# Solving the triangular systems of two DeltaNet heads together, with the keys' norms taken ahead

## The chip, the cores and the metric

The kernel runs on one core of a Trainium2 chip. The metric is the device time of one execution in microseconds (us). Each core has TensorE (PE, matrix products into PSUM), VectorE (DVE), ScalarE (ACT), GpSimd (POOL) and SyncE (SP, which issues the DMAs). Each engine works through its own instructions in the order in which they are written, and engines wait for each other by semaphores.

## The reference, cut to what matters

One layer of a diffusion backbone on 512 latent and 256 context tokens of width 1024. One projection feeds two mixers, a gated DeltaNet of 8 heads and an mLSTM of 4 heads, both run forward and backward in time; they are gated, projected, merged and normalised. The change touches the DeltaNet. Per head, chunk and direction it needs the inverse of a unit lower triangular matrix:

```python
kb = kc * bc[..., None]
a = jnp.where(strict, jnp.einsum('nbhid,nbhjd->nbhij', kb, kc) * dmask, 0.0)
eye = jnp.eye(CHUNK, dtype=a.dtype)
tinv = lax.linalg.triangular_solve(a + eye, jnp.broadcast_to(eye, a.shape),
                                   left_side=True, lower=True)
u = jnp.einsum('nbhij,nbhjd->nbhid', tinv, vc * bc[..., None])
w = jnp.einsum('nbhij,nbhjd->nbhid', tinv, kb * jnp.exp(gcum)[..., None])
```

The keys k are divided by their norm before this (`l2norm`).

## The kernel before

The kernel takes chunks of 128 tokens: 6 of them, 2 of context and 4 latent (NCH = 6). The projections are dense products of 128x128 weights with 512 or 256 tokens, three fp32r products each (weights and activations are split into a high and a low part: `whs`/`wls`, `hh`/`hl`). ScalarE makes `whs` and VectorE `wls` for each block of weights. They fill TensorE most of the time, and the DeltaNet's steps are set between them.

The steps of one DeltaNet head are generators. `dn_kv` transposes the keys and values and makes the squared norms `ssk`, and from them C1 (the factor beta over the squared norm), C1E and nk. `dn_scores` makes the decay mask Dm (ScalarE's exponential of a TensorE product) and multiplies it with the products q k and k k; the latter, GD, overwrites Dm. Dm has two buffers; that of head h is free after the last product with GD in `dn_prepb(h)`. `dn_prepa2` inverts the diagonal blocks: each 128x128 matrix has 4 diagonal blocks of 32x32, so that a head has 6 x 4 = 24 blocks in each of 2 directions. VectorE multiplies the blocks of GD with C1 into `TC2` (8 products), two 32x32 stream transposes lay them out in `TL` with one block on each partition, and 30 substitution steps follow, each a product into `tmp` and a subtraction. Here 64 partitions hold the blocks (32 for each direction), and the other 64 hold the same blocks for the odd columns: `Z` has the even columns on partitions 0 to 63 and the odd on 64 to 127. ScalarE copies to this layout and back, GpSimd clears the upper part and sets the diagonal, and two more transposes leave the inverses in `TL`.

`dn_prepb` places the inverted blocks from TL into A1, B1 and XF (ScalarE and GpSimd) and puts together the inverse of the 128x128 matrix by products on TensorE: first A1 with GD, then W with B1, then the same with A2 and B2. `dn_scan` runs 6 steps over the chunks in both directions; `dn_norm` and `dn_out` end the head.

The loop over the heads puts a stage together: `dn_prepb(h)` beside `dn_kv(h + 1)`, then the scan of h beside `dn_prepa2(h + 1)` and `dn_scores(h + 2)`, and beside all of it dense work (`z_dense`, `ml_dense`, `ml_gate`, `qkv(h + 3)`) and at odd heads `ml_mix`, the mLSTM.

What is recorded in this way is not yet the program. A `Recorder` takes each instruction with its reads and writes, and `_arrange` sets the order on each engine: a list scheduling over a table of costs in ns (`_cost`), by how urgent an instruction is for TensorE (`_needs`), in 8 rounds of which it keeps the one that its costs like best. So a change in one step can move instructions of every engine. All instructions that were recorded have line 460 in the profile; tiles tell them apart.

Of the kernel before, what the change touches and what calls it, by code (L numbers as in the profile page):

```python
# [21 lines left out]
NCH = TT // P  # L22
# [466 lines left out]
def conv_col(ch):  # L489
    return ch * P if ch < NCC else SEG + (ch - NCC) * P  # L490


def hybrid(tc, x, c, ctx_in, c_ctx, ada_w, ada_b, norm_g, w_in, conv_w, a_log, dt_bias,
           norm_a_g, i_bias, f_bias, norm_b_g, w_pa, w_pb, w_out, final_g, out):
    nc = tc.nc
# [9 lines left out]
    hs = ExitStack()  # L505
# [51 lines left out]
    cpow = const.tile([P, 16], F32, name="cpow")[:, 0:2]  # L557
# [46 lines left out]
    nc = rec  # L604
# [8 lines left out]
    gch, gcl, bcol, NEGC, EKD, EGL, KW, BB, EM, SCL = [rec.wrap(t) for t in gcols]  # L613
# [13 lines left out]
    pt = psm()  # L627
# [18 lines left out]
    junk = sp.tile([P, D], F32, name="junk")  # L646
# [57 lines left out]
    for half in range(2):  # L704
# [288 lines left out]
    def zeroed(name, shape):  # L993
        t = mx.tile(shape, F32, name=name)
        nc.gpsimd.memset(t, 0.0)
        return t

    TL = zeroed("TL", [P, 32, 32])
    TC2 = zeroed("TC2", [64, 32, 32])
    A1 = zeroed("A1", [P, NCH, P])  # L1000
    B1 = zeroed("B1", [P, NCH, P])
    A2, B2 = A1, B1
# [27 lines left out]
    heads = {}  # L1030
# [33 lines left out]
    def transposes(src, cols, pt=None):  # L1064
        pt = pt or psm()
        for i, cl in enumerate(cols):
            nc.tensor.transpose(pt[:, P * i:P * i + P], src[:, cl:cl + P], ident)
        return pt

    BATCH = ((0, 3), (3, 6))  # L1070

    def dn_kv(h):

        r = heads[h]
        k, v = r["k"], r["v"]
        KTm = mx.tile([P, NCH, P], F32, tag="KT", name="KTm", bufs=2)
        Vt = mx.tile([P, NCH, P], F32, tag="Vt", name="Vt", bufs=2)
        ssk = mx.tile([P, NCH], F32, tag="ssk", name="ssk", bufs=2)
        for b0, b1 in BATCH:
            pt = transposes(k, [conv_col(ch) for ch in range(b0, b1)], psl())  # L1080
            n = b1 - b0
            nc.scalar.copy(KTm[:, b0:b1, :], pt[:, 0:n * P].rearrange("p (c i) -> p c i", i=P))
            for ch in range(b0, b1):
                nc.scalar.activation(Vt[:, ch, :], KTm[:, ch, :], AF.Square, accum_out=ssk[:, ch:ch + 1])
            yield Y_T
        rk2 = mx.tile([P, NCH], F32, tag="rk2", name="rk2", bufs=2)
        nk = mx.tile([P, NCH], F32, tag="nk", name="nk", bufs=2)
        nc.vector.tensor_scalar(ssk, ssk, EPS, None, op0=ALU.add)
        nc.vector.reciprocal(rk2, ssk)
        nc.gpsimd.tensor_tensor(nk, ssk, cpow[:, 1:2].broadcast_to([P, NCH]), op=ALU.pow)  # L1090
        C1 = mx.tile([P, 2, NCH], F32, tag="C1", name="C1", bufs=2)
        C1E = mx.tile([P, 2, NCH], F32, tag="C1E", name="C1E", bufs=2)
        for d in range(2):
            nc.vector.tensor_tensor(C1[:, d, :], bcol[:, :, 8 * d + h], rk2, op=ALU.mult)
            nc.vector.tensor_tensor(C1E[:, d, :], C1[:, d, :], EKD[:, :, 8 * d + h], op=ALU.mult)
        yield Y_T
        for b0, b1 in BATCH:
            pt = transposes(v, [conv_col(ch) for ch in range(b0, b1)], psl())
            for ch in range(b0, b1):
                nc.scalar.activation(Vt[:, ch, :], pt[:, P * (ch - b0):P * (ch - b0) + P], AF.Copy, scale=nk[:, ch:ch + 1])  # L1100
            yield Y_T
        r.update(KT=KTm, Vt=Vt, C1=C1, C1E=C1E)

    def dn_scores(h):

# [39 lines left out]
            yield Y_T  # L1145
        r.update(GD=GD, PD=PD)

    def dn_prepa2(h):
        r = heads[h]
        C1, GD = r["C1"], r["GD"]  # L1150

        for b in range(4):
            sl = slice(32 * b, 32 * b + 32)
            for d in range(2):
                nc.vector.tensor_tensor(TC2[32 * d:32 * d + 32, 6 * b:6 * b + 6, :], GD[sl, :, sl],
                                        C1[sl, d, :].unsqueeze(2).broadcast_to([32, NCH, 32]), op=ALU.mult)
        nc.vector.transpose(TL[0:32], TC2[0:32].rearrange("p l i -> p i l"))
        nc.vector.transpose(TL[32:64].rearrange("p r c -> p c r"), TC2[32:64].rearrange("p l i -> p i l"))

        nc.scalar.copy(TL[64:128], TL[0:64])  # L1160
        Z = mx.tile([P, 32, 16], F32, tag="Z", name="Z")
        nc.scalar.copy(Z[0:64], TL[0:64, :, 0:32:2])
        nc.scalar.copy(Z[64:128], TL[0:64, :, 1:32:2])
        nc.vector.memset(Z[64:128].rearrange("p a b -> p (a b)")[:, 16:512:33], 0.0)
        tmp = mx.tile([P, 128], F32, tag="tmp", name="tmp")
        for s in range(1, 31):
            m, w = 31 - s, (s + 1) // 2
            tv = tmp[:, 0:m * w].rearrange("p (r c) -> p r c", c=w)
            nc.vector.tensor_tensor(tv, TL[:, s + 1:32, s:s + 1].broadcast_to([P, m, w]),
                                    Z[:, s:s + 1, 0:w].broadcast_to([P, m, w]), op=ALU.mult)  # L1170
            nc.vector.tensor_tensor(Z[:, s + 1:32, 0:w], Z[:, s + 1:32, 0:w], tv, op=ALU.subtract)
            if s % 5 == 0:
                yield Y_I
        nc.scalar.copy(TC2[:, :, 0:32:2], Z[0:64])
        nc.scalar.copy(TC2[:, :, 1:32:2], Z[64:128])
        nc.gpsimd.affine_select(out=TC2, in_=TC2, pattern=[[1, 32], [-1, 32]], compare_op=ALU.is_gt,
                                fill=0.0, base=0, channel_multiplier=0)
        nc.gpsimd.memset(TC2.rearrange("p a b -> p (a b)")[:, 0:1024:33], -1.0)
        nc.vector.transpose(TL[0:64].rearrange("p l s -> p s l"), TC2)
        nc.vector.transpose(TL[64:128].rearrange("p l s -> p s l"), TC2.rearrange("p r c -> p c r"))  # L1180
        yield Y_I

    def dn_prepb(h):
        r = heads[h]
        k, q, C1, GD, PD = r["k"], r["q"], r["C1"], r["GD"], r["PD"]
        Xf, Xb, XfT, XbT = TL[0:32], TL[96:128], TL[64:96], TL[32:64]

        def placep(dst, src, b, b0=0, b1=NCH):
            sl = slice(32 * b, 32 * b + 32)
# [7 lines left out]
        for b in range(4):  # L1197
            sl = slice(32 * b, 32 * b + 32)
# [11 lines left out]
        for b in (1, 2):  # L1210
            sl = slice(32 * b, 32 * b + 32)
# [53 lines left out]
        pt = psm()  # L1265
# [264 lines left out]
    for h in range(HA):  # L1530
        j = h // 2
        last = h + 1 == HA
        p1, p2 = [(W_B, dn_prepb(h))], [(W_S + W_N, seq(dn_scan(h), dn_norm(h), dn_out(h)))]
        if h + 1 < HA:
            p1.append((W_KV, dn_kv(h + 1)))
            p2.append((W_A2, dn_prepa2(h + 1)))
        if h + 2 < HA:
            p2.append((W_E, dn_scores(h + 2)))
        dn, wd = [par(*p1), par(*p2)], sum(w for w, _ in p1 + p2)
        de, cost = [], 0.0  # L1540
        if h + 1 < HA:
# [26 lines left out]
    nc, ps_d, ps_l, ps_s, ps_o, wpool, cvp, hh, hl, whs, wls, ya_d, yb_d, sg_d, gate_d, cpow = plain  # L1568
# [35 lines left out]
    for n in range(KT):  # L1604
        terms = []
        for i, ((ph, pl), wsrc) in enumerate(((parts[1], w_pa[0]), (parts[0], w_pb[0]))):
# [4 lines left out]
            w = load_w(wsrc, P * n)  # L1611
# [34 lines left out]
    n = [0] * NLC  # L1646
    for i, c0, c1 in pieces:
        wh, wl = wo[c0 // HD]
        cs, w0, w = slice(c0, c1), c0 % HD, c1 - c0
        ps = psd()[:, 0:w]  # L1650
        m = 0
# [12 lines left out]
        r = rf[:, i:i + 1]  # L1664
# [34 lines left out]
```

## Time and profile before

| | |
|---|---|
| median of 3 runs | 1000.65 us (1000.18 to 1001.67) |
| profiled execution | 1000.94 us, its span 999.2 us |
| TensorE busy | 956.1 us (96%) |
| VectorE busy | 741.1 us (74%) |
| ScalarE busy | 537.9 us (54%) |
| GpSimd busy | 214.5 us (21%) |
| mean granted TensorE clock | 0.989 of 2.4 GHz |

Times in the rows are us unless marked ns. A tile's buffer numbers are left out, so TC is TC2, A is A1, and so on. An fp32 product of TensorE stands as two records, an fp32r product or a transpose as one. The granted clock is 1.00 at 2.4 GHz and 0.5 at 1.2 GHz; a share between them is a mean over a stretch.

### The profile page before, as it was taken

The page shows a single profiled execution, that of the slowest core. Times are in us where ns is not written, and L with a number is a line of the kernel's source. Part 1 is how long each engine was busy: PE and PEld are TensorE (multiplying, and loading weights), DVE is VectorE, ACT ScalarE, POOL GpSimd, SP SyncE. Part 2 cuts the span into 40 slices and gives each one's busy share as a digit, 9 for nine tenths or more (in the row PEclk, how much of TensorE's full clock was granted, in tenths as well). Part 3 has the DMA queues.
Part 4 walks back from the last instruction along what each step waited for, and adds up shares of the span by engine and source line. Part 5 has one row for each costly group of instructions (what it writes and reads, how often), then busy time and mean ns, then how long its engine had stood idle before and what let it go on. Part 6 is the DMA issues. An engine that isn't in the chain of part 4 may idle for free.

```text
span 999.2 us, 15245 instructions
## 1 busy us (share of the span) xinstructions
PE 956.1 (96%) x5504; PEld 816.6 (82%) x5504; DVE 741.1 (74%) x1694; ACT 537.9 (54%) x1181; POOL 214.5 (21%) x292
## 2 busy tenths in 40 slices
PE   4999999999999899999989999999999999999996
PEld 2288889778889689988878998887998888788875
DVE  5798877887868978887888787887878445543544
ACT  6467564864775475485456558536545434422322
POOL 2201130411430151142023124103014000011131
PEclk9999999999999899999998999999999999999999
DMA  9821321533411231332114024214245148654462
GB/s 274 265 64 43 88 65 43 148 106 85 117 44 43 74 84 43 86 95 65 43 32 127 22 64 118 62 32 112 80 91 115 46 109 251 182 148 135 141 175 84
DMA packets 133104, 99.93 MB, mean 100 GB/s; under 512 B 6488, under 2 KB 113155, under 8 KB 133029
## 3 DMA queue, kind: packets, MB, share of 16 engines
q1 hardware_dynamic: 133029, 98.96, 35.9%
q8 instruction: 43, 0.70, 0.3%
q14 instruction: 32, 0.26, 0.1%
HBM read 89.70 MB, written 9.24 MB: 99 GB/s over the span
## 4 chain that ended last, share of the span: by engine, by line
PE 81%; DVE 8%; DMA 5%; ACT 4%; issue 1%; POOL 1%; SPq 0%; POOLq 0%; DVEq 0%; ACTq 0%
PE psd L460 46%; PE psl L460 16%; PE pts L460 6%; PE psd L769 3%; PE psd L770 3%; PE psd L768 3%; PE ops L460 3%; PE psd L1654 2%; DMA raw<-in_w_out 1%; DVE TL L460 1%; DMA xt<-in_x 1%; DMA yld<-ya_d 1%; DMA yld<-yb_d 1%; DVE xn L460 1%; DVE wls L460 1%
## 5 line engine op out<-in xcount | busy, mean ns | idle before, releaser
L460 PE MATMUL psd<-hh,whs 128*128 128x512 f32 (+1 forms) x696 | 273.6, 393 | 4.9 <-ACT pad L460 1.9
L460 PE MATMUL psd<-hh,wls 128*128 128x512 f32 (+1 forms) x696 | 259.2, 373 | 1.5 <-DVE wls L460 1.5
L460 PE MATMUL psd<-hl,whs 128*128 128x512 f32 (+1 forms) x696 | 258.6, 372 | 0.0
L460 PEld LDWEIGHTS psd<-hh,whs 128*128 128x128 f32 x696 | 132.2, 190 | 23.0 <-ACT pad L460 2.4
L460 PEld LDWEIGHTS psd<-hh,wls 128*128 128x128 f32 x696 | 131.7, 189 | 23.3 <-DVE wls L460 2.4
L460 PEld LDWEIGHTS psd<-hl,whs 128*128 128x128 f32 x696 | 132.3, 190 | 17.6 <-issue 0.9
L460 DVE TENSOR_TENSOR wls<-raw,whs 128x1024 fp32r<-128x1024 f32 x83 | 106.5, 1285 | 13.1 <-ACT whs L460 12.5
L460 ACT CAST whs<-raw 128x1024 fp32r<-128x1024 f32 x83 | 86.6, 1049 | 29.6 <-PE psd L460 16.8
L460 DVE STREAM_TRANSPOSE TL<-TC 32x1024 f32<-32x1024 f32 (+1 forms) x32 | 67.1, 2098 | 0.7 <-POOL TC L460 0.2
L460 DVE TENSOR_TENSOR Z<-Z,tmp 128x30 f32<-128x30 f32 (+7 forms) x240 | 62.4, 260 | 5.8
L460 DVE TENSOR_TENSOR tmp<-TL,Z 128x30 f32<-128x30 f32 (+7 forms) x240 | 61.7, 257 | 5.4
L460 ACT ACTIVATE ud<-pts,C1E 128x128 f32<-128x128 f32 x80 | 27.9, 366 | 55.4 <-PE pts L460 55.1
L460 PE MATMUL psd<-whs,hh 128*128 128x256 f32 x192 | 56.3, 294 | 0.0
L460 PE MATMUL psd<-wls,hh 128*128 128x256 f32 x192 | 54.6, 284 | 0.0
L460 PE MATMUL psd<-whs,hl 128*128 128x256 f32 x192 | 54.4, 284 | 0.0
L460 POOL TENSOR_SCALAR_AFFINE_SELECT Mm<-gch 128x384 fp32r<-128x384 f32 x32 | 22.7, 709 | 145.3 <-PE psl L460 110.7
L460 ACT ACT_TABLE_LOAD x40 | 51.3, 1283 | 1.5 <-PEq L1687 0.8
L753 ACT CAST whs<-raw 128x1024 fp32r<-128x1024 f32 x21 | 22.1, 1052 | 48.1 <-PE psd L769 44.0
L1615 POOL TENSOR_TENSOR yt<-yt 128x512 f32<-128x512 f32 x8 | 14.7, 1831 | 106.5 <-DVE yt L1613 71.4
L754 DVE TENSOR_TENSOR wls<-raw,whs 128x1024 fp32r<-128x1024 f32 x21 | 27.9, 1328 | 12.7 <-ACT whs L753 11.4
L460 POOL TENSOR_SCALAR_AFFINE_SELECT P<-PD 128x512 f32<-128x512 f32 x8 | 6.6, 827 | 142.6 <-PE ops L460 137.5
L460 PEld LDWEIGHTS psd<-wls,hh 128*128 128x128 f32 x192 | 36.6, 191 | 0.1
(299 smaller groups left out, 2217.0 us busy)
## 6 DMA issues: line engine op xcount, KB each, us to landing
raw<-in_w_in SPq DMA_DIRECT2D x80, 512.0 KB, 3.9
ada_t<-in_ada_w SPq DMA_DIRECT2D x16, 512.0 KB, 9.5
raw<-in_ada_w SPq DMA_DIRECT2D x8, 512.0 KB, 3.7
Qd<-rows_d SPq DMA_DIRECT2D x16, 256.0 KB, 4.2
raw<-in_w_pa SPq DMA_DIRECT2D x8, 512.0 KB, 3.8
raw<-in_w_pb SPq DMA_DIRECT2D x8, 512.0 KB, 3.9
raw<-in_w_out SPq DMA_DIRECT2D x8, 512.0 KB, 8.9
sg_d<-sg SPq DMA_DIRECT2D x11, 256.0 KB, 3.2
```

The source lines that it names most:

```text
L460: getattr(getattr(self.nc, s.eng), s.name)(*a, **k)
L753: nc.scalar.copy(wh, raw)
L754: nc.vector.tensor_tensor(wl, raw, wh.bitcast(F32), op=ALU.subtract)
L768: nc.tensor.matmul(o, wh[:, kt, :], rh[:, kt, t0:t1], start=kt == 0, stop=False)
L769: nc.tensor.matmul(o, wh[:, kt, :], rl[:, kt, t0:t1], start=False, stop=False)
L770: nc.tensor.matmul(o, wl[:, kt, :], rh[:, kt, t0:t1], start=False, stop=kt == KT - 1)
L1615: nc.gpsimd.tensor_tensor(terms[0], terms[0], terms[1], op=ALU.add)
L1654: nc.tensor.matmul(ps, a[:, kt, P * i:P * i + P], b[:, kt, w0:w0 + w], start=m == 0, stop=m == KT * 3 - 1)
```

## The change

`dn_prepa2` takes one or two heads. Each head has 64 partitions of `TL` (32 for each direction) and keeps whole columns, so that Z, the split by column parity and ScalarE's copies are gone; the substitution runs in place in TL, with `tmp` up to 240 columns wide. The blocks are laid out through `TX`. The two transposes at the end move into `dn_prepb`, from TL into TX, so that TL keeps a second head's inverses until its own `dn_prepb`.

The heads go as 0 alone, then 1 and 2, 3 and 4, 5 and 6, and 7 alone. At even h the loop solves h+1 and h+2 after `dn_scores(h + 2)`; at odd h it solves nothing. Since C1 of head h+2 is now needed a stage earlier, `dn_norms(h + 2)` transposes its keys only for their norms; `dn_kv` transposes them again later for the scan, without the norms. C1 and C1E have three buffers instead of two.

```diff
+    def dn_norms(h):
+
+        ssk = mx.tile([P, NCH], F32, tag="ssk", name="ssk", bufs=2)
+        for b0, b1 in BATCH:
+            pt = transposes(heads[h]["k"], [conv_col(ch) for ch in range(b0, b1)], psl())
+            for ch in range(b0, b1):
+                junk = mx.tile([P, P], F32, tag="u", name="junk", bufs=2)
+                nc.scalar.activation(junk, pt[:, P * (ch - b0):P * (ch - b0) + P], AF.Square, accum_out=ssk[:, ch:ch + 1])
+            yield Y_T
+        dn_factors(h, ssk)
+        yield Y_T
...
-    def dn_prepa2(h):
...
-        nc.scalar.copy(TL[64:128], TL[0:64])
-        Z = mx.tile([P, 32, 16], F32, tag="Z", name="Z")
-        nc.scalar.copy(Z[0:64], TL[0:64, :, 0:32:2])
-        nc.scalar.copy(Z[64:128], TL[0:64, :, 1:32:2])
...
+    def dn_prepa2(*hs):
+
+
+        n = 64 * len(hs)
+        nc.gpsimd.memset(TX[0:n, 24:32, :], 0.0)
+        for e, h in enumerate(hs):
+            C1, GD = heads[h]["C1"], heads[h]["GD"]
+            heads[h]["inv"] = e
+            for b in range(4):
+                sl = slice(32 * b, 32 * b + 32)
+                for d in range(2):
+                    q = 64 * e + 32 * d
+                    nc.vector.tensor_tensor(TX[q:q + 32, 6 * b:6 * b + 6, :], GD[sl, :, sl],
+                                            C1[sl, d, :].unsqueeze(2).broadcast_to([32, NCH, 32]), op=ALU.mult)
+            q = 64 * e
+            nc.vector.transpose(TL[q:q + 32], TX[q:q + 32].rearrange("p l i -> p i l"))
+            nc.vector.transpose(TL[q + 32:q + 64].rearrange("p r c -> p c r"), TX[q + 32:q + 64].rearrange("p l i -> p i l"))
+        tmp = mx.tile([P, 240], F32, tag="tmp", name="tmp")
         for s in range(1, 31):
-            m, w = 31 - s, (s + 1) // 2
...
+            m = 31 - s
+            tv = tmp[0:n, 0:m * s].rearrange("p (r c) -> p r c", c=s)
+            nc.vector.tensor_tensor(tv, TL[0:n, s + 1:32, s:s + 1].broadcast_to([n, m, s]),
+                                    TL[0:n, s:s + 1, 0:s].broadcast_to([n, m, s]), op=ALU.mult)
+            nc.vector.tensor_tensor(TL[0:n, s + 1:32, 0:s], TL[0:n, s + 1:32, 0:s], tv, op=ALU.subtract)
...
     def dn_prepb(h):
...
-        Xf, Xb, XfT, XbT = TL[0:32], TL[96:128], TL[64:96], TL[32:64]
+        z = TL[64 * r["inv"]:64 * r["inv"] + 64]
+        nc.vector.transpose(TX[0:64].rearrange("p l s -> p s l"), z)
+        nc.vector.transpose(TX[64:128].rearrange("p l s -> p s l"), z.rearrange("p r c -> p c r"))
+        Xf, Xb, XfT, XbT = TX[0:32], TX[96:128], TX[64:96], TX[32:64]
...
-            p2.append((W_A2, dn_prepa2(h + 1)))
-        if h + 2 < HA:
-            p2.append((W_E, dn_scores(h + 2)))
+        if h + 2 < HA:
+            early = [dn_norms(h + 2), dn_scores(h + 2), dn_prepa2(h + 1, h + 2)] if h % 2 == 0 else [dn_scores(h + 2)]
+            p2.append((3 * Y_T + W_E + W_A2 if h % 2 == 0 else W_E, seq(*early)))
+        elif h + 1 < HA:
+            p2.append((W_A2, dn_prepa2(h + 1)))
```

How the scheduler's order moves is shown at two places. First VectorE ahead of the solve that `dn_prepb(3)` needs. Before, the block products of head 3 alone (TC) are made right after its factors C, and the scores of head 4 are not among the rows ahead:

```order
L460 TENSOR_TENSOR C_3713<-bcol,rk_3639 128x6
L460 TENSOR_TENSOR TC_617<-Dm,C_3713 32x192 x8
L460 SCALAR_TENSOR_TENSOR cvv<-pad_117,cwt,cvv 128x772
L460 STREAM_TRANSPOSE TL<-TC_617 32x1024
L460 SCALAR_TENSOR_TENSOR Sn<-Sn,EGL,pts 128x128 x2
L460 TENSOR_TENSOR wls<-raw,whs 128x1024
L460 SCALAR_TENSOR_TENSOR R<-pts,NEGC,Vt 128x128 x2
L460 STREAM_TRANSPOSE TL<-TC_617 32x32x32
```

Now the score products of head 4 (Dm from psl, which is GD) stand straight ahead of its block products (TX), and these ahead of the solve of heads 3 and 4:

```order
L460 TENSOR_TENSOR wls<-raw,whs 128x1024
L460 SCALAR_TENSOR_TENSOR Sn<-Sn,EGL,pts 128x128
L460 TENSOR_TENSOR Dm<-psl,Dm 128x384 x2
L460 TENSOR_TENSOR TX<-Dm,C_3720 32x192
L460 SCALAR_TENSOR_TENSOR R<-pts,NEGC,Vt 128x128 x2
L460 TENSOR_TENSOR TX<-Dm,C_3720 32x192 x7
L460 STREAM_TRANSPOSE TL<-TX 32x1024
L460 TENSOR_TENSOR wls<-raw,whs 128x1024
L460 STREAM_TRANSPOSE TL<-TX 32x32x32
L460 TENSOR_TENSOR kw<-psl,KW 128x384 x2
```

So the scores of the later head have moved in front of the earlier head's solve. The second place is TensorE at `dn_prepb(1)`. Before, transposes (mk, cvk), products of the mLSTM (mq) and dense products (psd) stand between the products with A and B:

```order
L460 MATMUL psd<-hh,wls 128x512
L460 MATMUL psl<-A_637,Dm 128x128 x3
L460 MATMUL psl<-ident,mk 128x128 x3
L460 MATMUL psl<-ident,cvk 128x128 x3
L460 MATMUL psl<-A_637,Dm 128x128 x3
L460 MATMUL psd<-hh,whs 128x512
L460 MATMUL psd<-hl,whs 128x512
L460 MATMUL psl<-B_642,W 128x128 x3
L460 MATMUL psl<-mq,mk 128x128 x4
L460 MATMUL psl<-B_642,W 128x128 x3
```

Now they follow the transposes of head 0's output (on), and one another, almost alone:

```order
L460 MATMUL psd<-hh,wls 128x512
L460 MATMUL psl<-ident,on 128x128 x4
L460 MATMUL psl<-A_639,Dm 128x128 x6
L460 MATMUL psl<-B_647,W 128x128 x6
L460 MATMUL psd<-hh,whs 128x512
L460 MATMUL psd<-hl,whs 128x512
L460 MATMUL psl<-A_639,Dm 128x128 x3
L460 MATMUL psl<-ident,cvv 128x128 x3
L460 MATMUL psl<-mV,kw 128x257
L460 MATMUL psl<-A_639,Dm 128x128 x3
```

The dense work that stood between them has moved to other places of the queue.

## Rows read from the trace of the kernel before

**Rows 1.** The page, busy time of each engine, its share of the span, instructions:
```profile
PE 956.1 (96%) x5504; PEld 816.6 (82%) x5504; DVE 741.1 (74%) x1694; ACT 537.9 (54%) x1181; POOL 214.5 (21%) x292
```
**Rows 2.** The page, the chain that ended last, shares of the span:
```profile
PE 81%; DVE 8%; DMA 5%; ACT 4%; issue 1%; POOL 1%; SPq 0%; POOLq 0%; DVEq 0%; ACTq 0%
```
**Rows 3.** Stretch of the scans: length, busy us of each engine, clock, DMA:
```profile
175.00:775.00 600.00, 582.41 (x3591) 513.79 (x3591) 499.08 (x1214) 360.27 (x885) 152.98 (x219) 0.99 0.30 79
```
**Rows 4.** Two stretches with a low clock (the third number from the end):
```profile
275.00:350.00 75.00, 68.88 (x389) 60.54 (x388) 61.20 (x176) 42.19 (x92) 14.51 (x22) 0.93 0.20 54
500.00:550.00 50.00, 44.25 (x256) 38.60 (x256) 43.78 (x91) 30.42 (x90) 15.13 (x24) 0.93 0.29 80
```
**Rows 5.** Waits of TensorE, 175 to 775 us: us, times, longest:
```profile
PE psl L460 <- DVE A L460: 5.6, 4, 2.7
PE psl L460 <- DVE Z L460: 3.1, 1, 3.1
```
**Rows 6.** VectorE, groups by shape: count, busy us, mean ns, idle before:
```profile
L460 DVE TENSOR_TENSOR wls<-raw,whs 128x1024 fp32r<-128x1024 f32 x83 | 106.5, 1285 | 13.1 <-ACT whs L460 12.5
L460 DVE STREAM_TRANSPOSE TL<-TC 32x1024 f32<-32x1024 f32 x16 | 33.8, 2115 | 0.3
L460 DVE SCALAR_TENSOR_TENSOR cvk<-pad,cwt,cvk 128x772 f32<-128x772 f32 x32 | 33.5, 1047 | 2.2 <-ACT cvk L460 1.9
L460 DVE STREAM_TRANSPOSE TL<-TC 64x1024 f32<-64x1024 f32 x16 | 33.3, 2082 | 0.4 <-POOL TC L460 0.2
L460 DVE SCALAR_TENSOR_TENSOR R<-pts,NEGC,Vt 128x128 f32<-128x128 f32 x80 | 25.1, 346 | 15.0 <-PE pts L460 14.4
L460 DVE TENSOR_TENSOR TC<-Dm,C 32x192 f32<-32x192 f32 x64 | 24.8, 387 | 1.1
L460 DVE TENSOR_SCALAR wts<-wts,BB 128x128 f32<-128x128 f32 x32 | 9.4, 347 | 0.1
L460 DVE TENSOR_TENSOR kw<-psl,KW 128x384 f32<-128x384 f32 x16 | 8.2, 548 | 1.0 <-PE psl L460 0.9
L460 DVE TENSOR_TENSOR tmp<-TL,Z 128x120 f32<-128x120 f32 x24 | 7.3, 304 | 0.5
L460 DVE TENSOR_TENSOR tmp<-TL,Z 128x30 f32<-128x30 f32 x16 | 3.5, 216 | 0.3
```
**Rows 7.** ScalarE, groups by shape, the copies around a solve:
```profile
L460 ACT COPY Z<-TL 64x512 f32<-64x512 f32 x16 | 10.5, 659 | 0.2
L460 ACT COPY TC<-Z 64x512 f32<-64x512 f32 x16 | 10.5, 655 | 13.8 <-DVE Z L460 13.6
L460 ACT COPY TL<-TL 64x1024 f32<-64x1024 f32 x8 | 8.4, 1046 | 10.5 <-DVE TL L460 10.5
```
**Rows 8.** GpSimd, groups by shape, the select after a solve:
```profile
L460 POOL TENSOR_SCALAR_AFFINE_SELECT TC<-TC 64x1024 f32<-64x1024 f32 x8 | 10.7, 1343 | 80.8 <-ACT TC L460 80.8
```
**Rows 9.** TensorE in order of time: start, length, records (an A product has two):
```profile
273.63 0.39 PE L460 MATMUL psd<-hh,whs 128*128 128x512 f32 x1
273.86 0.39 PE L460 MATMUL psd<-hl,whs 128*128 128x512 f32 x1
...
276.82 0.28 PE L460 MATMUL psd<-hh,wls 128*128 128x256 f32 x1
276.94 0.83 PE L460 MATMUL psl<-A,Dm 128*128 128x128 f32 x6
277.61 0.49 PE L460 MATMUL psl<-ident,cvv 128*128 128x128 f32 x3
```
**Rows 10.** VectorE in order of time, seven block products of head 7:
```profile
705.71 2.54 DVE L460 TENSOR_TENSOR TC<-Dm,C 32x192 f32<-32x192 f32 x7
```
**Rows 11.** TensorE in order of time, first A and last B products of head 2:
```profile
356.88 0.83 PE L460 MATMUL psl<-A,Dm 128*128 128x128 f32 x6
...
368.45 0.92 PE L460 MATMUL psl<-B,W 128*128 128x128 f32 x6
```

More of the change, by code (lines that the diff above doesn't have):

```diff
@@ L998, in hybrid @@
     TL = zeroed("TL", [P, 32, 32])
-    TC2 = zeroed("TC2", [64, 32, 32])
+    TX = zeroed("TX", [P, 32, 32])
     A1 = zeroed("A1", [P, NCH, P])
@@ L1070, in hybrid, with dn_factors @@
     BATCH = ((0, 3), (3, 6))
+    def dn_factors(h, ssk):
+        rk2 = mx.tile([P, NCH], F32, tag="rk2", name="rk2", bufs=2)
+        nk = mx.tile([P, NCH], F32, tag="nk", name="nk", bufs=2)
+        nc.vector.tensor_scalar(ssk, ssk, EPS, None, op0=ALU.add)
+        nc.vector.reciprocal(rk2, ssk)
+        nc.gpsimd.tensor_tensor(nk, ssk, cpow[:, 1:2].broadcast_to([P, NCH]), op=ALU.pow)
+        C1 = mx.tile([P, 2, NCH], F32, tag="C1", name="C1", bufs=3)
+        C1E = mx.tile([P, 2, NCH], F32, tag="C1E", name="C1E", bufs=3)
+        for d in range(2):
+            nc.vector.tensor_tensor(C1[:, d, :], bcol[:, :, 8 * d + h], rk2, op=ALU.mult)
+            nc.vector.tensor_tensor(C1E[:, d, :], C1[:, d, :], EKD[:, :, 8 * d + h], op=ALU.mult)
+        heads[h].update(C1=C1, C1E=C1E, nk=nk)
+    def dn_norms(h):
[8 more added lines that the diff above has]
+        yield Y_T
     def dn_kv(h):
@@ L1077, in dn_kv @@
         Vt = mx.tile([P, NCH, P], F32, tag="Vt", name="Vt", bufs=2)
-        ssk = mx.tile([P, NCH], F32, tag="ssk", name="ssk", bufs=2)
+        if "C1" not in r:
+            ssk = mx.tile([P, NCH], F32, tag="ssk", name="ssk", bufs=2)
         for b0, b1 in BATCH:
@@ L1082, in dn_kv @@
             nc.scalar.copy(KTm[:, b0:b1, :], pt[:, 0:n * P].rearrange("p (c i) -> p c i", i=P))
-            for ch in range(b0, b1):
-                nc.scalar.activation(Vt[:, ch, :], KTm[:, ch, :], AF.Square, accum_out=ssk[:, ch:ch + 1])
+            if "C1" not in r:
+                for ch in range(b0, b1):
+                    nc.scalar.activation(Vt[:, ch, :], KTm[:, ch, :], AF.Square, accum_out=ssk[:, ch:ch + 1])
             yield Y_T
[L1086 to L1095, printed above, removed]
+        if "C1" not in r:
+            dn_factors(h, ssk)
+        nk = r["nk"]
         yield Y_T
@@ L1101, in dn_kv @@
             yield Y_T
-        r.update(KT=KTm, Vt=Vt, C1=C1, C1E=C1E)
+        r.update(KT=KTm, Vt=Vt)
     def dn_scores(h):
@@ L1146, in dn_scores @@
         r.update(GD=GD, PD=PD)
-    def dn_prepa2(h):
[L1149 to L1158, printed above, removed]
-        nc.scalar.copy(TL[64:128], TL[0:64])
-        Z = mx.tile([P, 32, 16], F32, tag="Z", name="Z")
-        nc.scalar.copy(Z[0:64], TL[0:64, :, 0:32:2])
-        nc.scalar.copy(Z[64:128], TL[0:64, :, 1:32:2])
-        nc.vector.memset(Z[64:128].rearrange("p a b -> p (a b)")[:, 16:512:33], 0.0)
-        tmp = mx.tile([P, 128], F32, tag="tmp", name="tmp")
-        for s in range(1, 31):
-            m, w = 31 - s, (s + 1) // 2
[L1168 to L1171, printed above, removed]
@@ new lines, in dn_prepa2 @@
+    def dn_prepa2(*hs):
[6 more added lines that the diff above has]
+                sl = slice(32 * b, 32 * b + 32)
+                for d in range(2):
+                    q = 64 * e + 32 * d
[5 more added lines that the diff above has]
+        tmp = mx.tile([P, 240], F32, tag="tmp", name="tmp")
+        for s in range(1, 31):
+            m = 31 - s
[3 more added lines that the diff above has]
+            nc.vector.tensor_tensor(TL[0:n, s + 1:32, 0:s], TL[0:n, s + 1:32, 0:s], tv, op=ALU.subtract)
@@ L1172, in dn_prepa2 @@
             if s % 5 == 0:
                 yield Y_I
-        nc.scalar.copy(TC2[:, :, 0:32:2], Z[0:64])
-        nc.scalar.copy(TC2[:, :, 1:32:2], Z[64:128])
-        nc.gpsimd.affine_select(out=TC2, in_=TC2, pattern=[[1, 32], [-1, 32]], compare_op=ALU.is_gt,
+        nc.gpsimd.affine_select(out=TL[0:n], in_=TL[0:n], pattern=[[1, 32], [-1, 32]], compare_op=ALU.is_gt,
                                 fill=0.0, base=0, channel_multiplier=0)
-        nc.gpsimd.memset(TC2.rearrange("p a b -> p (a b)")[:, 0:1024:33], -1.0)
@@ L1179, in dn_prepa2 @@
-        nc.vector.transpose(TL[0:64].rearrange("p l s -> p s l"), TC2)
-        nc.vector.transpose(TL[64:128].rearrange("p l s -> p s l"), TC2.rearrange("p r c -> p c r"))
+        nc.gpsimd.memset(TL[0:n].rearrange("p a b -> p (a b)")[:, 0:1024:33], -1.0)
         yield Y_I
```

## The prediction

> **What bounds the kernel now.** I read the page's engine shares first: TensorE is busy for 956.1 of 999.2 us, VectorE for 741.1 [rows 1]. Then the chain that ended last, 81% of it TensorE and 8% VectorE [rows 2]. So the kernel is bound by TensorE's own work, and a change can win only where TensorE waits, and loses wherever it adds a wait or a product. How much could be won is read from the stretch in which all the heads' scans run, 175 to 775 us: TensorE is busy for 582.41 of 600 us [rows 3], so 17.6 us are idle. Some more is lost to its clock: in 275 to 350 and in 500 to 550 us the mean granted clock is 0.93 [rows 4], that is 7% of 125 us, 8.8 us. Of the idle time the list of waits gives 5.6 us to the first products of the prepb steps ("A") and 3.1 us to VectorE still inside a substitution ("Z"), together 8.7 us [rows 5]. The other 8.9 us are many waits of 1 us and less. So at most 26 us of 1000 are at stake on the side of the gain.
>
> **What the change does to each engine.** The order of the changed kernel has 18 transposes more on TensorE (6 each for heads 2, 4 and 6) and nothing less. A transpose issues every 0.12 to 0.16 us [rows 9], so they cost 2 to 3 us, all of it on the path; I take 2.
>
> VectorE: one step of the substitution takes 304 ns for 120 columns and 216 for 30 [rows 6], about 187 ns plus 0.98 ns a column. A solve has 60 of them. Split by column parity it covers 2,600 columns for each of the two kinds, with whole columns 4,960 (the sum of s times 31-s for s from 1 to 30). So a solve takes 60 x 0.187 + 2 x 2,600 x 0.00098 = 16.3 us before and 20.9 us after, and there are 5 after (head 0; 1 and 2; 3 and 4; 5 and 6; 7) for 8 before: 130 us become 105, 26 us less. The 64 products into the block layout and the 32 transposes stay as many. ScalarE loses the copies around Z: 1.05 + 2 x 0.66 + 2 x 0.66 us for each of 8 solves [rows 7], 29 us. The squares of the keys are moved, not added. GpSimd's selects go from 8 to 5 of about 1.34 us [rows 8]. No DMA is added; SP issues the same 253. All this is off the path unless TensorE waits for it, so none of it counts by itself.
>
> **Where the path gets longer.** Before, the solve of head h+1 starts from scores that were made a stage earlier, and prepb(h+1) needs nothing of head h+2. After, the solve of heads h+1 and h+2 (h even) starts only when the scores of h+2 exist, and these wait for a Dm buffer that prepb(h) gives back. Both solves' results leave TL together, so prepb(h+1) now waits for: scores of h+2, their 8 block products, two transposes, the long solve, the select, two more transposes. In the order VectorE's rows show it (front part). I add up what stands on VectorE from the second score product of h+2 to the first A product of h+1, and what TensorE has to do meanwhile.
>
> prepb(1): VectorE has 8 block products of 0.387, 4 transposes of 2.1, the solve of 20.9, 3 weight splits of 1.285, 8 scan steps (R, Sn) of 0.346, 2 products kw of 0.548 [rows 6], and six small ones that I put at kw's length: 3.1 + 8.4 + 20.9 + 3.9 + 2.8 + 1.1 + 3.3 = 43.4 us. The select lies beside the last weight split, ScalarE's placements beside the product "on". TensorE has, between the same two places, 78 dense products of 512 columns at 0.23 us, 48 of 256 at 0.12, 29 fp32 products of 128 columns at 0.22 and 16 transposes at 0.12 [rows 9]: 17.9 + 5.8 + 6.4 + 1.9 = 32.0 us. It waits 11.4 us.
>
> prepb(3), counted alike: 3.1 + 8.4 + 20.9 + 2 x 1.285 + 6 x 0.346 + 4 x 0.548 + 5 convolution steps of 1.047 + 8 wts of 0.347 + 5 small ones = 50.0 us against 94, 48, 28 and 22 on TensorE: 21.6 + 5.8 + 6.2 + 2.6 = 36.2. It waits 13.8 us. prepb(5): six weight splits and nine small ones, 57.0 us, against 166, 48, 28 and 19: 52.5 us, a wait of 4.5.
>
> These are upper ends for VectorE: seven block products stand in 2.54 us [rows 10], 0.363 each instead of 0.387, so neighbours overlap a little. I take 10, 12 and 2: 24 us. The lower end is VectorE 15% shorter throughout, 5 + 6 + 0 = 11 us.
>
> Inside prepb, TensorE had filler before: from the first A product to the last B product it took 11.6 us at head 2 [rows 11]. This is a chain over VectorE and ScalarE that the change leaves as it is. In the new order little dense work is left for it at heads 1 and 5: 20 products, 2 to 3 dense ones and some transposes, about 6 us, so some 5.5 and 5 us of waiting more; at head 3 57 dense products cover it. Sum 10.5, bounds 0 (filler comes late and still fits) and 14.
>
> Sum against the profiled execution's 1000.94 us (span 999.2, median of the runs 1000.65): + 2 transposes, + 34.5 new waits (24 and 10.5), - 8.7 waits of the old kind, which go since single solves hang on nothing new, + 1.5 for the clock, - 2.5 since VectorE is light in the odd heads' stages, where nothing is solved, and part of the small waits goes. 1027.7, **1028 us**.
>
> The clock's 1.5: three pauses of the old kind cost 8.8 us [rows 4, 5], about 3 us each; three places with longer pauses stay, so I take three times 3.4. The low clock stands in the two stretches that hold these pauses. The Trainium skill, page "TensorE: Matmul & The Clock Gate", section "HAM oscillation", says that a TensorE that idles between bursts falls to half clock and starts each burst cold. The trace agrees at its three pauses; by the rule the two waits inside prepb would each bring a fall too, and the sum would be some 6 us more, 1034.
>
> **Queued behind the added wait.** On TensorE everything behind the A products: dense work of the next weights. On ScalarE the placements from TX stand ahead of the next weight casts, on VectorE the two transposes from TL ahead of the next splits; so the next dense work starts late too. That is in the waits above, since TensorE can't use it earlier.
>
> **Rivals.**
> (a) Faster: VectorE's load is what makes TensorE wait, and 26 us less of it takes away waits of all kinds. For it: VectorE is busy for 61 of 75 us and 44 of 50 us in the two bad stretches [rows 4]. If half of the 17.6 and 8.8 us goes: 1000.9 + 2 - 13 = 990. It decides if the chain of the pair fits beside TensorE's work, that is if VectorE needs 32 us and not 43 at prepb(1). Against: the counts, and that TensorE runs its instructions as they are written, so that filler from elsewhere can't step in. The Trainium skill ("VectorE: DVE Perf Modes", "Rules for kernel authors") says to lower the number of VectorE operations; 180 fewer at 187 ns are 34 us, less 8 for the added columns. It speaks for this rival, and the rows agree on the price. Chance 0.10.
> (b) Nothing: the new waits just take the place of the old (17.6 and 8.8 stay), with 2 us of transposes paid by a lighter VectorE: 1000 to 1002. Chance 0.04.
> (c) Slower, but milder: only the chains of heads 1 and 3 are late (10 and 12), and nothing inside prepb waits: 1000.9 + 2 + 22 - 8.7 - 2.5 = 1014. For it: before, the order hid just such chains. Chance 0.22.
> (d) Worse: the order lets the late dense work pile up, TensorE runs at half clock through each pause (10 us more) and prepb(5) waits its whole 4.5 and 5: 1045. Chance 0.12.
>
> **How the numbers follow.** The forecast, 1018 to 1038, has 0.52. The range reaches to 1005, which takes in (c), and to 1043, which takes in most of (d); left out are (a), (b) and the top of (d), under 0.2. Less than 0.2% (2 us) can't be told from no change: faster 0.10, same 0.04, slower 0.86.
>
> **What would show it.** Waits "psl <- DVE A" on TensorE of 10 us and more just ahead of the first A products of heads 1 and 3, with VectorE without a gap before them, and little or none ahead of heads 2, 4, 6 and 7. Five solves of 20 to 22 us of steps. Transposes of keys x66. The granted clock down at three places. VectorE busy for about 715 us, ScalarE for about 508. Wrong would be: no wait at A above 5 us (then (a) or (b)), or long waits at other places.

## The result, and the profile after

The changed kernel takes 1028.55 us (median of 4 runs, 1026.51 to 1029.39), the kernel before 1000.41 in the same comparison: 1.0277 times as long, 95% interval 1.0258 to 1.0296. The forecast was 1028 us. The profiled execution took 1026.51 us, its span is 1024.5 us, 25.3 more than before.

The page's engine row and chain of the changed kernel, against [rows 1, 2]:

```profile
PE 964.2 (94%) x5522; PEld 821.3 (80%) x5522; DVE 726.8 (71%) x1506; ACT 504.3 (49%) x1139; POOL 211.0 (21%) x291
PE 79%; DVE 9%; DMA 5%; ACT 4%; issue 2%; POOL 1%; POOLq 0%; SPq 0%; DVEq 0%; ACTq 0%
```

VectorE, ScalarE and GpSimd have less to do, and the kernel is slower. TensorE has 8.1 us more of work and 17.2 us more of idleness (span less busy: 60.3 against 43.1). Where, the stretches show (columns as in [rows 3]: length, busy us of each engine, granted clock, DMA):

```profile
175.00:775.00 600.00, 569.32 (x3507) 501.09 (x3505) 470.88 (x1016) 313.88 (x806) 136.74 (x204) 0.97 0.27 73
245.00:295.00 50.00, 38.62 (x211) 31.85 (x211) 45.39 (x107) 22.98 (x63) 10.25 (x18) 0.93 0.27 69
445.00:475.00 30.00, 18.20 (x74) 13.42 (x73) 25.41 (x52) 14.34 (x40) 8.24 (x15) 0.66 0.27 79
630.00:665.00 35.00, 28.30 (x145) 23.30 (x144) 27.79 (x60) 18.22 (x45) 12.55 (x16) 0.95 0.30 83
```

In the first row TensorE idles for 30.7 us, where it idled for 17.6 [rows 3]. The other three are the stretches around prepb(1), prepb(3) and prepb(5): 11.4, 11.8 and 6.7 us idle, 29.9 of the 30.7. They are also the stretches with a low clock. The waits of TensorE from 175 to 775 us (us, times, longest), against [rows 5]:

```profile
PE psd L460 <- DVE wls L460: 8.8, 3, 4.3
PE psd L460 <- ACT sz L460: 6.6, 2, 5.6
PE psl L460 <- DVE A L460: 5.0, 3, 2.4
PE psd L460 <- ACT og L460: 2.2, 1, 2.2
PE psl L460 <- ACT Vt L460: 2.0, 2, 1.0
```

The largest waits are not for A, as forecast, but of dense products (psd) for a weight split (wls) or for ScalarE's read of a finished product (sz). What stands behind these names is read in order of time. First at prepb(1) of the changed kernel, all engines (start, length, engine, operation; in brackets the idle time before and its releaser):

```profile
248.76 0.32 DVE L460 TENSOR_TENSOR TL<-TL,tmp 128x150 f32<-128x150 f32 x1
249.00 1.22 DVE L460 TENSOR_TENSOR wls<-raw,whs 128x1024 fp32r<-128x1024 f32 x1
250.13 0.32 DVE L460 TENSOR_TENSOR tmp<-TL 128x168 f32<-128x168 f32 x1
...
250.27 0.50 PE L460 MATMUL psd<-hh,wls 128*128 128x512 f32 x1 [4.32 <-DVE wls L460]
```

The split stands in VectorE's queue behind 12 operations of the pair's solve, and a dense product that has nothing to do with the solve waits 4.3 us for it. The same at prepb(3), where the way is longer:

```profile
454.33 0.19 DVE L460 TENSOR_TENSOR TL<-TL,tmp 128x30 f32<-128x30 f32 x1
454.44 0.74 DVE L460 SCALAR_TENSOR_TENSOR sz<-psl,prm,sz 128x512 f32<-128x512 f32 x1
...
455.21 0.32 SPq L460 DMA_DIRECT2D ya_d<-sz  x1
...
457.29 0.60 ACT L460 ACTIVATE sz<-psd 128x512 f32<-128x512 f32 x1 [6.25 <-DMA ya_d<-sz]
...
457.94 0.80 PE L460 MATMUL psd<-hh,whs 128*128 128x512 f32 x1 [5.63 <-ACT sz L460]
```

At 454.33 the last step of the solve begins. Only behind it does VectorE make the output of head 2 (sz), whose input TensorE had transposed by 445. The DMA that stores it frees the buffer, ScalarE reads a finished dense product into that buffer, and with its PSUM bank free TensorE goes on: the 5.6 us put down to ScalarE are VectorE's solve, three steps further back.

The length of the chain is read from the same trace, for heads 1, 3 and 5. The first line of each pair has the two score products of the later head, the second the first A products of the earlier one:

```profile
236.39 1.23 DVE L460 TENSOR_TENSOR Dm<-psl,Dm 128x384 f32<-128x384 f32 x2
282.48 0.91 PE L460 MATMUL psl<-A,Dm 128*128 128x128 f32 x6 [0.94 <-DVE sz L460]
...
411.84 1.01 DVE L460 TENSOR_TENSOR Dm<-psl,Dm 128x384 f32<-128x384 f32 x2
461.57 1.62 PE L460 MATMUL psl<-A,Dm 128*128 128x128 f32 x6 [2.41 <-DVE A L460]
...
595.58 1.23 DVE L460 TENSOR_TENSOR Dm<-psl,Dm 128x384 f32<-128x384 f32 x2 [0.39 <-PE psl L460]
656.00 0.83 PE L460 MATMUL psl<-A,Dm 128*128 128x128 f32 x6
```

From the end of the score products to the first A product it takes 44.9, 48.7 and 59.2 us, where the prediction counted 43.4, 50.0 and 57.0.

The groups of the changed kernel that answer to [rows 6, 8, 9], by shape (count, busy us, mean ns, idle before):

```profile
L460 DVE STREAM_TRANSPOSE TX<-TL 64x1024 f32<-64x1024 f32 x16 | 33.1, 2066 | 1.9 <-POOL TL L460 1.6
L460 DVE TENSOR_TENSOR tmp<-TL 128x240 f32<-128x240 f32 x6 | 2.4, 406 | 0.2
L460 DVE TENSOR_TENSOR tmp<-TL 64x240 f32<-64x240 f32 x4 | 1.6, 400 | 0.1
L460 DVE TENSOR_TENSOR tmp<-TL 128x30 f32<-128x30 f32 x6 | 1.2, 195 | 0.1
L460 PE MATMUL psl<-ident,cvk 128*128 128x128 f32 x66 | 10.6, 272 | 0.0
L460 POOL TENSOR_SCALAR_AFFINE_SELECT TL<-TL 128x1024 f32<-128x1024 f32 x3 | 4.7, 1572 | 43.6 <-DVE TL L460 43.6
```

On 128 partitions a step costs 195 ns at 30 columns and 406 at 240; on 64 partitions, in the single solves of heads 0 and 7, 400 at 240. The groups with all widths together, in the changed kernel, e2_single and e6_short below:

```profile
L460 DVE TENSOR_TENSOR tmp<-TL 128x30 f32<-128x30 f32 (+19 forms) x150 | 50.0, 334 | 3.8
```

```profile
L460 DVE TENSOR_TENSOR tmp<-TL 64x30 f32<-64x30 f32 (+14 forms) x240 | 78.2, 326 | 4.8
```

```profile
L460 DVE TENSOR_TENSOR tmp<-TL 64x30 f32<-64x30 f32 (+7 forms) x240 | 59.9, 249 | 5.2
```

The first of these groups mixes 90 steps on 128 partitions with 60 on 64; the other two are on 64 throughout. So a solve of 60 steps is 60 x 0.334 = 20.0 us in the changed kernel and 19.7 in e2_single, and in the steps themselves the second head comes almost free of charge.

### The profile page after: what moved, and what is told of

The parts are those of the page before. It is cut to its first block, busy times and chain, and to the rows that moved or that the text cites. A ratio compares the mean times of both kernels' runs of the same rounds, so it can differ in the third digit from the quotient of the medians.

```text
span 1024.5 us, 15047 instructions
## 1 busy us (share of the span) xinstructions
PE 964.2 (94%) x5522; PEld 821.3 (80%) x5522; DVE 726.8 (71%) x1506; ACT 504.3 (49%) x1139; POOL 211.0 (21%) x291
## 4 chain that ended last, share of the span: by engine, by line
PE 79%; DVE 9%; DMA 5%; ACT 4%; issue 2%; POOL 1%; POOLq 0%; SPq 0%; DVEq 0%; ACTq 0%
PE psd L460 43%; PE psl L460 18%; PE pts L460 5%; PE psd L769 3%; PE psd L768 3%; PE psd L770 3%; PE ops L460 3%; DVE TL L460 2%; DVE tmp L460 2%; PE psd L1675 2%; DMA raw<-in_w_out 1%; DMA yld<-yb_d 1%; DVE TX L460 1%; DMA yld<-ya_d 1%; DMA raw<-in_w_in 1%
## 5 line engine op out<-in xcount | busy, mean ns | idle before, releaser
L460 PE MATMUL psd<-hh,wls 128*128 128x512 f32 (+1 forms) x696 | 262.0, 378 | 8.8 <-DVE wls L460 8.8
L460 PE MATMUL psd<-hl,whs 128*128 128x512 f32 (+1 forms) x696 | 261.6, 376 | 0.0
L460 DVE TENSOR_TENSOR wls<-raw,whs 128x1024 fp32r<-128x1024 f32 x83 | 108.6, 1312 | 19.3 <-ACT whs L460 19.0
L460 DVE TENSOR_TENSOR tmp<-TL 128x30 f32<-128x30 f32 (+19 forms) x150 | 50.0, 334 | 3.8
L460 DVE TENSOR_TENSOR TL<-TL,tmp 128x30 f32<-128x30 f32 (+19 forms) x150 | 50.0, 333 | 3.9
L460 POOL TENSOR_SCALAR_AFFINE_SELECT Mm<-gch 128x384 fp32r<-128x384 f32 x32 | 20.2, 630 | 146.6 <-PE psl L460 110.8
L460 ACT COPY pad<-psd 128x512 f32<-128x512 f32 (+1 forms) x40 | 19.7, 501 | 54.4 <-PE psd L460 48.0
L460 DVE SCALAR_TENSOR_TENSOR R<-pts,NEGC,Vt 128x128 f32<-128x128 f32 x80 | 25.4, 346 | 23.6 <-PE pts L460 22.9
L460 DVE SCALAR_TENSOR_TENSOR Sn<-Sn,EGL,pts 128x128 f32<-128x128 f32 x64 | 20.6, 344 | 26.4 <-PE pts L460 25.6
L460 PEld LDWEIGHTS psl<-A,Dm 128*128 128x128 f32 x192 | 26.2, 199 | 13.8 <-ACT XF L460 4.0
```

The lines of the kernel that those rows point to most:

```text
L460: getattr(getattr(self.nc, s.eng), s.name)(*a, **k)
```

## The experiments

The theories: A, the pair's solve starts from scores made in the same stage, and this chain is late; B, the longer steps load VectorE; C, the order is drawn anew by any change; D, the norms cost it. Ratios are to the kernel before, run beside each.

**The chain cut (e1_twin).** Both halves of the solve take the earlier head's blocks.

```diff
-            C1, GD = heads[h]["C1"], heads[h]["GD"]
+            C1, GD = heads[hs[0]]["C1"], heads[hs[0]]["GD"]
```

> Both halves of the pair's solve take the blocks of the earlier head (h+1), so that the solve no longer needs the scores and norms of head h+2; every instruction is still issued, and the later head's inverses are those of the wrong head. Theory A (the chain: prepb(h+1) is late because the pair's solve starts from the scores of h+2): 996 to 1006 us, the waits and the half-clock pieces ahead of prepb(1), prepb(3) and prepb(5) gone. Theory B (the longer whole-column solve and the load that it puts on VectorE): the same 60 steps of 128 partitions, so 1020 to 1030. Theory C (any change of the recorded work draws another order, better or worse by chance): no direction, 1015 to 1040.

Measured: 990.82 us, ratio 0.9904 (0.9886 to 0.9922). The same instructions are issued, and the time falls by 1.0277 - 0.9904 = 3.7%, some 37 us, to less than the kernel before. So the dependence on the later head is worth 37 us, and the rest of the change is a gain of 10. VectorE is as busy as in the changed kernel (725.3 against 726.8 us), so B, which wanted 1020 or more, falls for the pair. From 175 to 775 us these waits of TensorE are left, nearly all at prepb(1):

```profile
PE psl L460 <- DVE Dm L460: 5.9, 1, 5.9
PE psl L460 <- DVE A L460: 2.4, 1, 2.4
PE psl L460 <- DVE W L460: 2.3, 2, 1.9
PE psl L460 <- DVE wts L460: 0.2, 1, 0.2
```

**Whole columns without pairs (e2_single).** The stages of the kernel before with the new `dn_prepa2`.

```diff
-            early = [dn_norms(h + 2), dn_scores(h + 2), dn_prepa2(h + 1, h + 2)] if h % 2 == 0 else [dn_scores(h + 2)]
-            p2.append((3 * Y_T + W_E + W_A2 if h % 2 == 0 else W_E, seq(*early)))
+            p2.append((W_E, dn_scores(h + 2)))
...
+            p2.append((W_A2, dn_prepa2(h + 1)))
```

> The whole-column solve of one head at a time, in the stages of the kernel before, norms inside dn_kv, no Z and no copies of ScalarE. Theory A: the chain is longer by 4.6 us a head only, and nothing waits for a later head's scores: 1000 to 1010. Theory B: VectorE gets 8 solves of 20 to 21 us instead of 8 of 16.3, 30 to 37 us more than before, more than in the changed kernel: 1028 or more. Theory C: anywhere from 1000 to 1040.

Measured: 1026.08 us, 1.0255 (1.0238 to 1.0272). Theory A missed this by 16 us and more; B was near. The places are not those of the changed kernel. These stretches of e2_single lie around prepb(2), prepb(4) and prepb(6):

```profile
330.00:365.00 35.00, 23.60 (x106) 18.32 (x105) 31.02 (x76) 16.87 (x51) 8.11 (x11) 0.80 0.16 46
525.00:550.00 25.00, 15.95 (x75) 13.52 (x74) 19.05 (x30) 19.46 (x62) 6.54 (x13) 0.73 0.30 88
700.00:740.00 40.00, 29.89 (x179) 26.34 (x178) 32.44 (x67) 21.87 (x74) 12.31 (x19) 0.83 0.30 86
```

TensorE idles for 11.4, 9.1 and 10.1 us there. These solves run in the odd stages, beside `ml_mix`. In the first stretch, TensorE of e2_single in order of time:

```profile
338.27 0.94 PE L460 MATMUL psl<-cvk 128*128 128x128 f32 x6 [2.90 <-DVE PD L460]
344.33 1.09 PE L460 MATMUL psl<-ident,on 128*128 128x128 f32 x4 [5.12 <-DVE H L460]
```

PD and H are steps of the scores and of the mLSTM; on VectorE they stand between steps of the solve, which lasts until 347.4.

**Its length taken away (e6_short).** Half of the columns of each step.

```diff
-            tv = tmp[0:n, 0:m * s].rearrange("p (r c) -> p r c", c=s)
+            w = (s + 1) // 2
+            tv = tmp[0:n, 0:m * w].rearrange("p (r c) -> p r c", c=w)
```

> The single whole-column solves of e2_single with only the first half of each step's columns (the width (s+1)//2 of the kernel before, on 64 partitions): the later columns of each block are left unsolved. Still 60 steps a head, without Z and without ScalarE's copies. If e2_single is slow through the length of its solves (theory B): 993 to 1003, as the solve is as long as before and two copies shorter. If it is slow through the layout (TX taken for the blocks only after prepb(h) has read it, and two transposes of TL at the start of prepb): still 1018 to 1030.

Measured: 1002.10 us, 1.0018 (1.0004 to 1.0032). So 2.37 of the 2.55% of e2_single are the length of the steps, not the layout. VectorE is busy for 736.5 us instead of 770.3: 34 us less on an engine that is busy three quarters of the time gave 24 us. Whether a solve's own lateness or VectorE's load counts for more in this isn't separated.

**The norms alone (e3_norms).** The kernel before, with `dn_norms(h + 2)` ahead of `dn_scores(h + 2)` at even h.

```diff
-            p2.append((W_E, dn_scores(h + 2)))
+            early = [dn_norms(h + 2), dn_scores(h + 2)] if h % 2 == 0 else [dn_scores(h + 2)]
+            p2.append((3 * Y_T + W_E if h % 2 == 0 else W_E, seq(*early)))
```

> The kernel before with the norms of heads 2, 4 and 6 taken ahead by 18 more transposes, and nothing paired. Theory A: the transposes alone, 2 to 3 us on TensorE: 1002 to 1005. Theory B: as A. A theory D that the norms taken apart (their place ahead of the scores on TensorE and the squares on ScalarE) are a large part of the 28 us: 1012 or more.

Measured: 1003.58 us, 1.0037 (1.0023 to 1.0051), 2 to 5 us. D falls.

**The solve halved (e7_half).**

```diff
-        for s in range(1, 31):
+        for s in range(1, 31, 2):
```

> The changed kernel with every second substitution step left out (30 of the 60 operations of a solve, the others unchanged): the pair's solve is some 10 us shorter, the scores of head h+2 still come first. Theory A: the chain ahead of prepb(1), (3), (5) is 10 us shorter of about 37 that it costs in all, in three places: 998 to 1010. Theory that only the order of start matters and not the length: 1020 or more.

Measured: 1006.67 us, 1.0063 (1.0048 to 1.0078): 10 us out of each solve take 21 us from the whole. That fits a chain whose length counts as well as its start; but VectorE also has 51 us less to do (675.5 against 726.8), and this run alone doesn't tell the two apart.

**The chain begun earlier: first the buffer alone (e5_buffers), then with the place (e4_early).**

```diff
-        Dm = mx.tile([P, NCH, P], F32, tag="Dm", name="Dm", bufs=2)
+        Dm = mx.tile([P, NCH, P], F32, tag="Dm", name="Dm", bufs=3)
...
-                m = mx.tile([P, n, P], F32R, tag="Mm", name="Mm", bufs=2)
+                m = mx.tile([P, n, P], F32R, tag="Mm", name="Mm", bufs=1)
```

and in e4_early, besides:

```diff
-            early = [dn_norms(h + 2), dn_scores(h + 2), dn_prepa2(h + 1, h + 2)] if h % 2 == 0 else [dn_scores(h + 2)]
-            p2.append((3 * Y_T + W_E + W_A2 if h % 2 == 0 else W_E, seq(*early)))
+            if h % 2 == 0:
+                p1.append((3 * Y_T + W_E, seq(dn_norms(h + 2), dn_scores(h + 2))))
+                p2.append((W_A2, dn_prepa2(h + 1, h + 2)))
+            else:
+                p2.append((W_E, dn_scores(h + 2)))
```

> The changed kernel with the third Dm buffer and the single Mm buffer alone; the scores of head h+2 stay recorded beside the scan. Theory A with the recorded place as the cause (the chain starts late because its steps stand beside the scan): no gain, 1022 to 1034. Theory A with the buffer as the cause (the scores wait for the Dm that prepb(h) gives back): 992 to 1005.

> The changed kernel with the norms and scores of head h+2 recorded beside prepb(h) instead of beside its scan, a third Dm buffer so that they need not wait for prepb(h), and one Mm buffer instead of two to make room. Same pairs, same solves. Theory A: the chain starts about a scan earlier and the solve is done before TensorE gets to prepb(h+1): 993 to 1005, waits ahead of prepb(1), (3), (5) together under 8 us. Theory B: VectorE's work is the same: 1020 to 1030. Theory C: no direction.

Measured: 1023.32 us with the buffer alone, 1.0229 (1.0213 to 1.0246); 992.47 us with both, 0.9924 (0.9909 to 0.9939). The buffers alone give 5 us, with the place it is 35. So the recorded place is what matters; the early place without a third buffer wasn't tried, so that the buffer may be needed for it. In e4_early all waits of note are in the first of these two stretches, at prepb(1):

```profile
245.00:300.00 55.00, 44.47 (x256) 37.76 (x255) 50.80 (x104) 27.09 (x73) 19.16 (x21) 0.88 0.25 72
300.00:775.00 475.00, 474.83 (x3017) 427.38 (x3016) 376.65 (x838) 269.48 (x683) 111.29 (x171) 1.00 0.27 75
```

Of the 475 us after it TensorE idles for 0.2. The 10.5 us at prepb(1) are more than the 8 expected.

**Dense work moved to that wait (e8_filler, on top of e4_early), and the same in the kernel before (e11_filler_before).** G is the number of blocks of the gate columns in each stage.

```diff
-    G = [0, 2, 0, 0, 0, 2, 2, 4]
+    G = [4, 0, 0, 0, 0, 0, 2, 4]
```

> e4_early with dense work moved between stages: of the gate columns of the projection 4 blocks stand in stage 0 instead of none, none in stage 1 instead of 2, none in stage 5 instead of 2 (4 blocks are 96 products, some 22 us). e4_early still waits some 10 us and runs at half clock for 13.7 us ahead of and in prepb(1), the only long wait that is left. Theory A: TensorE has work there while the pair's chain runs: 978 to 988. Rival: the waits move to stage 1 or 5, from which work is taken: 990 to 998.

> The move of dense work of e8_filler alone, in the kernel before (8 single solves, parity split). If the gain of e8_filler is that of the move: 984 to 992. If it needs the pair (in the kernel before the waits stand ahead of prepb of even heads too, in the odd stages, from which work is taken): 998 to 1006.

Measured: 978.81 us, 0.9788 (0.9771 to 0.9804), for e8_filler; 998.36 us, 0.9987 (0.9970 to 1.0004), in the kernel before. The pair, its scores early and the filler in stage 0 make the best of the kernels run, 2.1% under the one before. Its row for the scans:

```profile
175.00:775.00 600.00, 598.56 (x3744) 531.39 (x3743) 485.10 (x1073) 344.88 (x875) 150.99 (x219) 1.00 0.29 80
```

1.4 us idle of 600, at the full clock throughout, where the kernel before had 17.6 [rows 3].

**Controls for the luck of an order (e9_slack_before, e10_slack_after).** One constant of the scheduler.

```diff
-    SLACK, AHEAD, ROUNDS = 100.0, 15000.0, 8
+    SLACK, AHEAD, ROUNDS = 150.0, 15000.0, 8
```

> A control: the kernel before with one constant of its scheduler changed (the time that it allows between an engine's end and TensorE's start, 150 ns for 100), which draws another order of the same instructions. Theory C (the 28 us could be the luck of a draw): differences of 10 us and more. Theory A: a draw moves the time by a few us only, 996 to 1006.

> The same constant in the changed kernel. Theory A: 1020 to 1036, as every draw has the scores of head h+2 ahead of the pair's solve. Theory C: 1010 or less, or 1045 and more.

Measured: 999.66 us, 0.9997 (0.9980 to 1.0014), and 1025.85 us, 1.0276 (1.0253 to 1.0300). One new draw of each left both where they were; as far as one draw can show it, theory C falls. In e10_slack_after TensorE meets its long waits, 10.5, 7.0 and 5.9 us, at the same three places, but under another name. Behind the first stands again an operation of VectorE (cvk) that was queued between steps of the solve:

```profile
PE psd L460 <- ACT pad L460: 23.8, 4, 10.5
...
277.36 0.24 DVE L460 TENSOR_TENSOR tmp<-TL 128x84 f32<-128x84 f32 x1
277.53 1.01 DVE L460 SCALAR_TENSOR_TENSOR cvk<-pad,cwt,cvk 128x772 f32<-128x772 f32 x1
...
278.63 0.59 ACT L460 COPY pad<-psd 128x512 f32<-128x512 f32 x1 [9.77 <-DVE cvk L460]
```

## Why the prediction was right

**The cause** was the one named, and the count of the chain held: 44.9, 48.7 and 59.2 us against 43.4, 50.0 and 57.0. Of the time, 37 us hang on the dependence on head h+2 (e1_twin), where the prediction had 34.5 of waits and 1.5 of clock; without it the change gains 10 us, where it had 11.2 given back by waits of the old kind and a lighter VectorE, less 2 for the transposes. Of the chain's links, the wait for a Dm buffer counted little: the buffers of e5_buffers, without the earlier place, give 5 us.

**The terms**, in the profiled executions. New waits: 15.5, 12 and 7 us forecast at heads 1, 3 and 5; 11.4, 11.8 and 6.7 measured. Old waits: 11.2 of the 17.6 us were to go; 0.8 are left outside the three places, so 16.8 went. Transposes: 2 forecast; by e3_norms 2 to 5 with their squares. Clock: 1.5 forecast, the smallest term and in proportion the one most mis-sized: TensorE's busy time rose by 8.1 us, and 2 to 3 of these are transposes [rows 9], so an estimate of 5 to 6 is left for work at 1.2 GHz. The longest low piece is at prepb(3), where TensorE was at the lower of its two levels from 449 to 469 us and busy for half of that, which is about 5 us of loss:

```profile
449.00:469.00 20.00, 10.12 (x31) 7.44 (x32) 16.80 (x33) 9.44 (x23) 5.37 (x8) 0.50 0.17 52
```

It fell after three waits of 1.0, 0.5 and 0.5 us, and stayed low through the wait of 5.6 us. The Trainium skill, page "TensorE: Matmul & The Clock Gate", section "HAM oscillation", lets each burst after an idle stretch start cold; the trace agrees in part, with 0.66 in 250 to 255 us, behind the wait of 4.3 us, but 1.00 in 280 to 290 us, where TensorE idles for 4.3 us in waits of 1.1 us and less. The 1034 us that the prediction gave by that rule had 6 us more for this, which for this term alone was nearer than 1.5. Idleness outside 175 to 775 us: none forecast, 4 us measured, 3 of them in one wait at 96.6 us (4.3 us, against 1.3 before), ahead of the first stage, which neither e1_twin, with the same pair, nor e10_slack_after, the same kernel in another order, has; that is the luck of an order. Sum: 2.5 + 29.9 - 16.8 + 5.6 + 4.1 = 25.3. So four terms were off by 4 to 6 us, two each way, and 1028 was luckier than its terms. Rival (d) doesn't add up either: the forecast with its 10 us of clock and 2.5 more at prepb(5) is 1040, not 1045, as the 5 us inside that prepb are in the forecast already.

**The sign was wrong.** The prediction wanted waits for A of 10 us and more, and said that no wait for A above 5 us would speak for rivals (a) or (b). The longest is 2.4 us, and it was neither. The step that failed is "That is in the waits above, since TensorE can't use it earlier": what is queued behind the solve on VectorE was thought late but harmless. The prediction looked only at what stands behind the A products. What TensorE comes to first are dense products ahead of them in its queue, whose splits and buffers stand in VectorE's queue between and behind the steps of the solve. The places were right, and the time lost is much the same (29.9 us against 34.5), but its name is another: wls, sz and A here, pad in e10_slack_after. A sign that would have held is idleness of TensorE while VectorE is in the pair's solve.

**VectorE** was to fall to about 715 us and fell to 726.8: the steps of the solves went from 124.1 to 100.0 us, 24 less where 26 were forecast. No one group holds the other 10 us: the times of all groups together fall by 23 us, from 790.2 to 767.0. The page counts time in which two records of VectorE overlap once, and neighbours overlap by 49 us before and by 40 after (the sums less 741.1 and 726.8); that is 9 of the 10, and why they overlap less stays open. ScalarE: 504.3, forecast 508.

**Rival (a)**, that a lighter VectorE makes the kernel faster (990 us), had the right price and lacked the condition: its time came in e1_twin and e4_early (991 and 992 us), where the chain is out of the way. Whether the lighter VectorE gives these 10 us, or ScalarE without the copies, isn't separated. The Trainium skill ("VectorE: DVE Perf Modes", "Rules for kernel authors") wants few VectorE operations, and these two runs agree with it; but the changed kernel has 188 operations of VectorE fewer than the kernel before and is slower, and e2_single has 8 fewer, 29 us more of work, and is slower too.

**Not seen** was that whole columns have a price even without pairs: e2_single is 26 us slower with solves of 19.7 us instead of 124.1 / 8 = 15.5. The prediction counted the length only in the chains of the pairs (which e7_half fits), and as free elsewhere. With the pair's dependence cut or its inputs early it is nearly free: the odd stages, where it hurts in e2_single, have no solve, and e1_twin and e4_early wait almost only at prepb(1).

## What to carry to other kernels

When two iterations of a loop are put into one batch, the first of them inherits what the second waits for; ask how early the later input can be made, before asking what the batch saves. Run a kernel without that dependence, whatever it then leaves out of the result: the time says what an earlier start could give (here 37 us, of which moving the inputs a step forward, with a third buffer, brought 35). Then put spare work for the bound engine where the one wait is left.

## What the runs showed of the hardware that was not expected

- A wait is named after its last link. The 5.6 us wait of TensorE for ScalarE came from VectorE by way of a DMA: 454.4 (VectorE), 455.2 (the DMA is issued), 457.3 (ScalarE), 457.9 us (TensorE).
- VectorE's in-place steps take nearly as long on 64 partitions as on 128 (400 and 406 ns at 240 columns), so the parity split that shortens a solve from 20 to 15.5 us and the second head compete for the same free partitions.
